# A two-layer hybrid trunk: calmer splitting ahead and top-k, a warmer start, and two embedding blocks moved between the last output products

## The chip, the cores and the metric

The kernel runs on one core of one Trainium2 chip. The metric is the device time of one launch in microseconds (us), from the chip's own timing. The kernel before takes 2018.87 us (median of 3 runs, 2017.33 to 2019.59). A core has a matrix engine (TensorE, PE in the profile), a vector engine (VectorE, DVE), an activation engine (ScalarE, ACT), GpSimd (POOL) and SyncE (SP), which here issues nearly all transfers (DMAs). Each engine runs its instructions in the order in which the program lists them.

## What is computed

Two decoder layers on a sequence of 1024 tokens of width 1024, all in float32. In outline:

```
for i in 0, 1:
    y = gla_mixer(x) if i == 0 else dsa_mixer(x)
    x = layer_norm(ALPHA * x + y) * ln_g[i] + ln_b[i]
    x = x + (p[i] @ ple_w[i]) * sigmoid(x @ ple_gate_w[i])

gla_mixer:  q, k, v, z, a = split(x @ w_in)          # 4 heads, chunks of 64 tokens
            g = log_sigmoid(a @ w_a2 + b_a) / 16;  G = cumsum(g) inside a chunk
            A = tril((q exp(G)) @ (k exp(-G)).T);  o = A @ v + (q exp(G)) @ S   # S: running state
            y = (rms_norm(o) * gn_g * silu(z)) @ w_out
dsa_mixer:  q, k, v, z, qi, ki, wi = split(x @ w_in)   # 16 heads, one k and v for all
            score = sum over 8 index heads of relu(qi @ ki.T) * wi, causal
            keep the top min(256, L/4) keys of each query;  attention on them
            y = (o * silu(z)) @ w_out
```

The term `p[i] @ ple_w[i]` is the per-layer embedding (`ple`): 256 by 1024 weights, done in eight blocks of 128 output columns.

## The kernel before

**Matmuls in three passes.** To keep float32 accuracy, every operand is split into a high part (rounded to the matrix engine's `fp32r`) and a low part (the rest): ACT makes the high part by a copy, DVE the low part by a subtraction (`split`, L395 and L403; for weights `Weights.step`, L180 and L182). A product is then three matmuls, high x high, low x high and high x low. A matmul is 128 by 128 weights against 512 columns.

**Weights.** `Weights` walks one list of keys, `seq`. A key's 128 x 1024 piece is loaded into one of two `wst` buffers (`loads`), split into the tiles `whi` and `wlo` (four buffers each) and handed out by `take`. The weights of layer 1 are used in both halves; `split_ahead` (L203 to L229) splits them once, during layer 0, in pieces of 512 columns: load into `pst` (two buffers), ACT copies to `phi` (L219), SP stores `phi`, DVE subtracts in place (L223), SP stores `pst`. Later the finished parts are simply loaded (`whole`).

**Halves and heads.** The sequence is cut into two halves of 512 tokens. Layer 0 goes through half 0 and half 1, each with four heads (`g_phase` makes the decays from log and exponential functions, `v_phase`, `qk_phase`, the core with its masks `Af`, `Ah`, `Al`, then `out_phase` with its sums in `y`), then the norm (`norm_steps`), the transposes and gate of `tail`. Between the halves stands the small head work of layer 1 for half 0 (`small_head`, `small_kv`, and the index scores with tiles `ix`, `rl`, `sc`). Layer 1 goes through the halves with 16 attention heads; in each head's slot stand projections (`q`, `z`) and output products (`o`) as cover for the softmax and its transposes (`sq`, `PT`, `ph`), whose sums are in the tile `o`. The last output products (`last_outs`, L333) need the last head's result `u`.

**What sets the order.** Nothing here is ordered by hand row by row. `Flow` keeps an estimated clock that is moved on by each matmul. A piece of side work is put in a heap with a due time (`at`, `after`, `chain`), or is fed by a pacer each time its gap has passed: `W.pace` for weights, `bg` for top-k (`topk_steps`) and rope tables, `bg3` for `split_ahead`, `feed_by` for the pieces of x. When the estimated clock passes a due time, the instruction is written into its engine's program at that place. So a different gap, a different `chain` time or a step issued earlier moves instructions against each other on DVE, ACT and SP, and each engine then runs them in that order whether or not the operands are there.

Of the kernel before, what the change touches and what calls it, by code (L numbers as in the profile page):

```python
# [23 lines left out]
HT = 512  # L24
# [113 lines left out]
class Weights:  # L138
# [15 lines left out]
    def step(self):  # L154
# [48 lines left out]
    def split_ahead(self, keys, pool):  # L203
# [11 lines left out]
        for i, (key, c) in enumerate(cuts):  # L215
# [49 lines left out]
def trunk_kernel(ctx, tc, x_tok, x_T, p_T, pos, freq, g_q, g_k, g_v, g_z, g_a, g_a2, g_ba, g_gn, g_o,  # L265
# [28 lines left out]
    def tail_keys(layer):  # L294
        return ([(("p", layer, c), ple_c[layer, c]) for c in range(2)]
                + [(("t", layer, b), gate_c[layer, b]) for b in range(NK)])
# [36 lines left out]
    last_outs = [("o", (6,), 1), ("o", (7,), 0), ("o", (7,), 1)]  # L333

    def unit_keys(u):
        if u[0] == "o":
            return [(("do", j, u[2]), d_o[j // 2, u[2], j % 2]) for j in u[1]]
# [156 lines left out]
    def g_phase(u, A):  # L494
# [16 lines left out]
        def soft(d):  # L511
            def f():
                act.activation(ta[:, d], ta[:, d], AF.Exp, scale=-1.0)
                act.activation(ta[:, d], ta[:, d], AF.Ln, bias=1.0)
            return f
# [29 lines left out]
        chain((0, lambda: None), (0.6, soft(0)), (1.1, soft(1)), (0.3, scan(0)), (1.1, scan(1)),  # L545
              (0.8, middle), (1.9, decays))
# [193 lines left out]
    def accumulate(parts, U, y, ch, rs=None, norm=None, ahead=1):  # L740
# [5 lines left out]
        for t, b in order:  # L746
# [16 lines left out]
            if norm is not None:  # L763
                norm(t)
            yield

    def out_phase(u, y, norm=None):
# [4 lines left out]
        for ch in range(2):  # L772
            parts = [W.take(("o", u["h"], ch, 0)), W.take(("o", u["h"], ch, 1))]
            for i, _ in enumerate(accumulate(parts, U, y, ch, u["rs"], norm if ch else None)):
# [14 lines left out]
    def norm_steps(y, np_, eps):  # L789
# [6 lines left out]
        def norm(t):  # L796
# [14 lines left out]
            chain((0, stats), (2.0, apply))  # L811
        return norm, f_done

    def tail(layer, Pt, y, y_done, final, tp, xps, x_alloc, tmp):

        ple = [tp.tile([128, 4, HT], F32, tag="z", name="ple", bufs=2) for _ in range(2)]
# [13 lines left out]
        for c in range(2):  # L830
            hi, lo = W.take(("p", layer, c))
            for b in range(4):
                ps = pbank()
                n = 0
                for k in range(2):
                    ph, pl = Pt[k]
                    bs = slice(k * 512 + b * 128, k * 512 + b * 128 + 128)
                    for l, r in ((hi, ph), (hi, pl), (lo, ph)):
                        mm(ps, l[:, bs], r, n == 0, n == 5)
                        n += 1  # L840
                    if k == 0:
                        yield
                if c:
                    dve.tensor_copy(ple[c][:, b], ps)
                else:
                    act.activation(ple[c][:, b], ps, AF.Copy)
                yield
                if c == 1:
                    xpose(2 * b)
                    yield  # L850
                    xpose(2 * b + 1)
                    yield
        for b in range(NK):
            def ev(ps, b=b):
                sg = tmp()

                def gated():
                    dve.tensor_mul(sg, sg, ple[b // 4][:, b % 4])
# [270 lines left out]
    def start_half(half):  # L1129
# [9 lines left out]

        def feed():  # L1140
            load(0, 1)
            W.loads(W.ns + 1)
            load(1, 1)
            W.loads(W.ns + 2)
            for k in range(2, NK, 2):
                load(k, 2)
            if half == 0:
                nc.sync.dma_start(ba, g_ba)
# [3 lines left out]
            else:  # L1152
                yield
# [10 lines left out]
        return X, units, feed()  # L1164
# [583 lines left out]
```

## Time and profile before

| | before |
|---|---|
| median of 3 runs | 2018.87 us |
| the profiled execution | 2016.59 us |
| its span, first to last instruction | 2014.8 us |
| mean granted clock of TensorE | 0.993 |
| busy: PE, DVE, ACT, POOL | 97%, 74%, 52%, 3% |

The profiled execution lies 2.3 us below the median and 1.8 us above its span. The granted clock has two levels, 1.2 and 2.4 GHz, written as 0.5 and 1.0 in the records, so that a stretch with a mean of 0.83 has spent a third of its time at the lower one. A row of the timeline gives the start, the busy time of one instruction (or of a run of equal ones), the engine, the line, the operation, the tiles, and in brackets the idle time of the engine before it with what ended it.

### The profile page before, as it was taken

What the parts mean: (1) busy time and instruction counts of PE and PEld (TensorE: products, weight loads), DVE (VectorE), ACT (ScalarE), POOL (GpSimd) and SP (SyncE); (2) the same over time, 40 slices, a digit from 0 to 9 for tenths busy, and PEclk for the clock granted to TensorE, in tenths of its full rate; (3) what the DMA queues carried; (4) which work ended last, traced back from release to release, by engine and by line L of the source; (5) the groups of instructions that cost most, each with busy time, mean ns of one, the idle gap of its engine ahead of it and who ended that gap; (6) DMA issues with size and microseconds to landing.
All of it is one profiled execution on the core that took longest, in us unless ns stands there. A gap on an engine that the chain in (4) does not pass through costs nothing.

```text
span 2014.8 us, 26716 instructions
## 1 busy us (share of the span) xinstructions
PE 1963.4 (97%) x9016; PEld 1616.3 (80%) x9016; DVE 1487.6 (74%) x3037; ACT 1046.5 (52%) x1943; POOL 53.7 (3%) x111
## 2 busy tenths in 40 slices
PE   8999999999999999999999999999899999999999
PEld 6788788877777888888888887888778888888877
DVE  5667666687677797877867986777796887777863
ACT  5664646445465646464555676766442553434432
POOL 0000000010000000000100000000000000000000
PEclk9999999999999999999999999999999999999999
DMA  4557575657856565657667487877766998888864
GB/s 149 174 162 221 171 218 171 222 174 243 283 180 224 161 225 167 225 162 224 196 218 266 157 311 246 303 265 276 271 211 215 352 333 295 291 300 279 295 249 147
DMA packets 173947, 464.96 MB, mean 231 GB/s; under 512 B 20081, under 2 KB 20849, under 8 KB 167665
## 3 DMA queue, kind: packets, MB, share of 16 engines
q1 hardware_dynamic: 173808, 463.25, 68.4%
q8 instruction: 71, 1.16, 0.2%
q14 instruction: 68, 0.55, 0.1%
HBM read 331.18 MB, written 131.99 MB: 230 GB/s over the span
## 4 chain that ended last, share of the span: by engine, by line
PE 81%; DVE 7%; ACT 5%; DMA 4%; issue 2%; SPq 0%; POOL 0%; POOLq 0%; ACTq 0%; DVEq 0%
PE pb L58 59%; PE o L58 8%; PE U L58 6%; PE S L58 5%; DMA xst<-x2s 1%; DMA wls<-pst 1%; DMA pst<-in_d_o 1%; DVE bn L803 1%; PE oT L62 1%; PE tr L58 1%; DVE wlo L182 1%; DVE sc L1018 1%; ACT whi L180 0%; DMA wst<-in_g_v 0%; DMA wlo<-wls 0%
## 5 line engine op out<-in xcount | busy, mean ns | idle before, releaser
L58 PE MATMUL pb<-x,whi 128*128 128x512 f32 x2272 | 709.9, 394 | 3.3 <-ACT whi L180 2.0
L58 PEld LDWEIGHTS pb<-x,whi 128*128 128x128 f32 x2272 | 417.2, 188 | 84.4 <-ACT whi L180 2.8
L58 PE MATMUL pb<-x,wlo 128*128 128x512 f32 x1136 | 444.2, 391 | 0.4 <-DVE wlo L182 0.4
L58 PE MATMUL pb<-whi,u 128*128 128x512 f32 x1024 | 347.2, 399 | 7.6 <-DVE u L395 4.2
L58 PEld LDWEIGHTS pb<-x,wlo 128*128 128x128 f32 x1136 | 213.8, 188 | 48.1 <-DVE wlo L182 2.3
L58 PEld LDWEIGHTS pb<-whi,u 128*128 128x128 f32 x1024 | 194.8, 190 | 49.9 <-DVE u L395 5.0
L58 PE MATMUL pb<-wlo,u 128*128 128x512 f32 x512 | 202.3, 395 | 0.0
L182 DVE TENSOR_TENSOR wlo<-wst,whi 128x512 fp32r<-128x512 f32 x232 | 154.8, 684 | 56.2 <-ACT whi L180 56.0
L180 ACT ACTIVATE whi<-wst 128x512 fp32r<-128x512 f32 x232 | 136.4, 621 | 47.2 <-DMA wst<-in_g_z 13.7
L219 ACT ACTIVATE phi<-pst 128x512 fp32r<-128x512 f32 x130 | 81.4, 626 | 126.2 <-DMA pst<-in_d_z 40.8
L1435 ACT ACTIVATE sq<-P,mx 128x128 f32<-128x128 f32 (+7 forms) x128 | 99.0, 774 | 83.8 <-DVE mx L1428 56.5
L1481 ACT ACTIVATE ph<-PT 128x512 fp32r<-128x512 f32 (+1 forms) x160 | 93.7, 601 | 65.7 <-PE o L58 50.4
L58 PE MATMUL S<-kT,q 128*128 128x512 f32 (+2 forms) x576 | 121.8, 343 | 0.0
L1479 DVE TENSOR_TENSOR PT<-PT,ph 128x512 fp32r<-128x512 f32 (+1 forms) x160 | 101.5, 648 | 20.6 <-ACT ph L1481 20.6
L58 PEld LDWEIGHTS S<-kT,q 128*128 128x128 f32 x576 | 100.6, 188 | 17.8 <-DVE mx L1428 0.7
L58 PEld LDWEIGHTS pb<-wlo,u 128*128 128x128 f32 x512 | 97.6, 191 | 18.8
L223 DVE TENSOR_TENSOR pst<-pst,phi 128x512 fp32r<-128x512 f32 x130 | 89.1, 685 | 29.8 <-ACT phi L219 29.8
L1084 ACT ACTIVATE tk<-sc,tki 128x768 f16<-128x768 f32 (+2 forms) x90 | 92.9, 1032 | 22.0 <-DVE tki L1093 15.9
L58 PE MATMUL o<-ph,vT 128*128 128x512 f32 (+2 forms) x384 | 102.4, 351 | 0.0
L1441 DVE STREAM_TRANSPOSE sq<-sq 128x128 f32<-128x128 f32 (+7 forms) x128 | 97.6, 768 | 3.1 <-ACT sq L1435 3.0
L58 PE MATMUL pb<-whi,x 128*128 128x512 f32 x256 | 89.1, 407 | 10.0 <-ACT whi L180 6.0
L709 ACT ACTIVATE junk<-o 128x512 bf16<-128x512 f32 x32 | 19.1, 597 | 139.8 <-DVE ot L707 135.3
(311 smaller groups left out, 3383.9 us busy)
## 6 DMA issues: line engine op xcount, KB each, us to landing
whi<-whs SPq DMA_DIRECT2D x130, 512.0 KB
wlo<-wls SPq DMA_DIRECT2D x130, 512.0 KB
sqd<-sq SPq DMA_DIRECT2D x192, 256.0 KB
PT<-sqd SPq DMA_DIRECT2D x48, 1024.0 KB
whs<-phi SPq DMA_DIRECT2D x130, 256.0 KB
wls<-pst SPq DMA_DIRECT2D x130, 256.0 KB
wst<-in_g_v SPq DMA_DIRECT2D x32, 512.0 KB
wst<-in_g_z SPq DMA_DIRECT2D x32, 512.0 KB
```

Of the source, the lines that this page charges most:

```text
L58: self.pe.matmul(out, lhsT, rhs, start=start, stop=stop)
L62: self.pe.transpose(out, in_, ident)
L180: self.nc.scalar.activation(hi[:, c], st[:, c], AF.Copy, scale=1.0 if gain is None else gain)
L182: self.nc.vector.tensor_sub(lo[:, c], st[:, c], hi[:, c].bitcast(F32))
L219: self.nc.scalar.activation(hi, st.bitcast(F32), AF.Copy)
L223: self.nc.vector.tensor_sub(st, st.bitcast(F32), hi.bitcast(F32))
L803: dve.bn_stats(st8[:, t, c], y[:, t, c * 512:c * 512 + 512])
L1084: act.activation(junk()[:, :n], scs[j], AF.Sign, bias=cand[:, j:j + 1].bitcast(F32), accum_out=cnt[:, j:j + 1])
L1435: act.activation(to, rows, AF.Exp, scale=-1.0, bias=mx, accum_out=sm[:, t:t + 1])
L1441: dve.transpose(x, x)
L1479: dve.tensor_sub(lo, lo.bitcast(F32), hi.bitcast(F32))
L1481: chain((0, lambda: act.activation(hi, lo.bitcast(F32), AF.Copy)), (0.8, second))
```

## The change

- **Start.** The first piece of x is split first, then the first two weight pieces in full (four steps of `W`, one before), and 22 matmuls of the identity by itself are put on PE ahead of the first real one. The bias tables of DVE come later.
- **`split_ahead`** issues the load of the next piece one step earlier. Its gap is 2.02 instead of 2.1, 2.43 while a core runs and 1.72 while a head's projections run; it stops while the small head work begins.
- **`g_phase`**: both exponentials, then both logarithms, instead of one pair after the other; the scans and decays are due a little later.
- **`norm`** is called for both column halves of `y`: the statistics of the first half are taken as soon as it is complete, not both at the end.
- **The `ple` of layer 1**: blocks 0 and 1 run as a unit of their own between the last two heads' output products; their weights lie in the two `wst` buffers. `tail` then makes six blocks instead of eight and ends with two more bare transposes.
- **Start of half 1**: x is loaded in four transfers of 512 KB spaced by 5 us of the estimated clock instead of five in a row together with two weight pieces, and is split from a later step on, at a gap of 2.2 instead of 1.2.
- **Top-k of half 1's rows**: gap 1.6 becomes 1.5 or 1.75, by the head; a pause is put at the last head. The product `z*inv` is made one group of the attention sum earlier, and the inputs of `ple` are loaded one head earlier.

```diff
             if not whole:
                 self.loads(n + 1)
-            self.parts[n] = tuple(self.pool.tile([128, 1024], F32R, tag=t, name=t, bufs=4) for t in ("whi", "wlo"))
+            tags = (("wst", 2),) * 2 if self.seq[n][0][:3] == ("p", 1, 0) else (("whi", 4), ("wlo", 4))
+            self.parts[n] = tuple(self.pool.tile([128, 1024], F32R, tag=t, name=t, bufs=b) for t, b in tags)
...
             self.nc.scalar.activation(hi, st.bitcast(F32), AF.Copy)
+            nxt = load(*cuts[i + 1]) if i + 1 < len(cuts) else None
             yield
             self.nc.sync.dma_start(there[0][:, c], hi.bitcast(F32))
-            nxt = load(*cuts[i + 1]) if i + 1 < len(cuts) else None
             self.nc.vector.tensor_sub(st, st.bitcast(F32), hi.bitcast(F32))
...
-    last_outs = [("o", (6,), 1), ("o", (7,), 0), ("o", (7,), 1)]
+    last_outs = [("o", (6,), 1), ("p",), ("o", (7,), 0), ("o", (7,), 1)]
...
-        chain((0, lambda: None), (0.6, soft(0)), (1.1, soft(1)), (0.3, scan(0)), (1.1, scan(1)),
-              (0.8, middle), (1.9, decays))
+        chain((0, lambda: None), (0.6, exps), (1.2, logs), (2.2, scan(0)), (0.7, scan(1)),
+              (1.0, middle), (1.9, decays))
...
+            dve.bn_stats(st8[:, t, ch], y[:, t, ch * 512:ch * 512 + 512])
+
             def stats():
-                for c in range(2):
-                    dve.bn_stats(st8[:, t, c], y[:, t, c * 512:c * 512 + 512])
                 dve.bn_aggr(mv[:, t], st8[:, t])
...
+        def fetch():
+            for k in range(0, NK, 2):
+                load(k, 2)
+                yield
...
             next(feeder)
-            W.step()
+            fl.need(lambda: X.t[0] is not None)
+            for _ in range(4):
+                W.step()
             next(feeder)
             feed_by(feeder, 0.0, 0.0)
+            idle = pp.tile([128, 512], F32, tag="o", name="o")
+            for _ in range(22):
+                nc.tensor.matmul(idle[:, 0:128], ident, ident, start=True, stop=True)
...
-                    bg3.set(W.split_ahead(later, lp), 2.1)
+                    bg3.set(W.split_ahead(later, lp), 2.02)
...
+            bg3.gap = 2.43
             steps = core_steps(u)
...
+            bg3.gap = 2.02 if h == GH - 1 else 1.72
...
+            nxt = start_half(1)
+            feed_by(nxt[3], fl.now + 2.0, 5.0)
+            bg3.due = max(bg3.due, fl.now + 7 * B)
...
-                    if i == 8:
-                        feed_by(nxt[2], fl.now + 0.7, 1.2)
+                    if i == 12:
+                        feed_by(nxt[2], fl.now + 0.7, 2.2)
...
-        bg.set(topk_steps([4, 5, 6, 7], scs, l1, tk, tk, on_act=(1, 2, 3)), 1.6)
+        bg.set(topk_steps([4, 5, 6, 7], scs, l1, tk, tk, on_act=(1, 2, 3)), 1.52)
...
+    def ple_block(parts, b, Pt, out, engine):
+
+        hi, lo = parts
+        ps = pbank()
+        n = 0
+        for k in range(2):
+            ph, pl = Pt[k]
+            bs = slice(k * 512 + b * 128, k * 512 + b * 128 + 128)
+            for l, r in ((hi, ph), (hi, pl), (lo, ph)):
+                mm(ps, l[:, bs], r, n == 0, n == 5)
+                n += 1
+            if k == 0:
+                yield
+        if engine is dve:
+            dve.tensor_copy(out, ps)
+        else:
+            act.activation(out, ps, AF.Copy)
+        yield
...
+        turns = iter(range(NK))
+        for b in range(done, 8):
+            if b % 4 == 0 or b == done:
+                parts = first if b < 4 and first else W.take(("p", layer, b // 4))
+            yield from ple_block(parts, b % 4, Pt, ple[b], dve if b >= 4 else act)
+            if b >= 4 + done // 2:
+                for _ in range(2):
+                    xpose(next(turns))
                     yield
...
+    def ple_unit(st):
+
+        st["pw"] = W.take(("p", 1, 0))
+        st["ple"] = [small_tile("qf") for _ in range(2)]
+        for b in range(2):
+            yield from ple_block(st["pw"], b, Pt, st["ple"][b], act)
...
+                if g == len(groups) - 2:
+                    z, inv = get(("z", h), ("inv", h))
+                    dve.tensor_mul(z, z, inv)
+                    st["zs", h] = z
...
+            bg.gap = 1.75 if h > 3 and h % 4 < 2 else 1.5
...
-            if h == 15:
-                Pt = load_p(1, half, lambda: small_tile("q", F32R, 4), 14.0)
+            if h == 14:
+                Pt = load_p(1, half, lambda: small_tile("q", F32R, 4), dur + 2.5)
```

How the rows move is shown at three places. The first is DVE at the start of half 1, in the first head's `k` projection (`m` is k times its decay, which the transposes `tr` on PE read; `pst` is the subtraction of `split_ahead`; `tkj` and `tki` belong to top-k). Before:

```order
L182 TENSOR_TENSOR wlo<-wst,whi 128x512
L1040 TENSOR_SCALAR tkj,tkf<-sc_103,tki 128x384
L223 TENSOR_TENSOR pst<-pst,phi 128x512
L589 TENSOR_TENSOR m<-pb,m 128x512
L658 COPY_PREDICATED Af_91<-cmask,tr 128x128
L631 SCALAR_TENSOR_TENSOR S<-R_97,mid,S 128x512
```

And now:

```order
L594 TENSOR_TENSOR m<-pb,m 128x512
L224 TENSOR_TENSOR pst<-pst,phi 128x512
L183 TENSOR_TENSOR wlo<-wst,whi 128x512
L1109 TENSOR_TENSOR tki<-tkf 128x2
L1110 SCALAR_TENSOR_TENSOR tki<-tki 128x2
L1112 TENSOR_SCALAR tki<-tki 128x2
L183 TENSOR_TENSOR wlo<-wst,whi 128x512
L1059 TENSOR_SCALAR tkj,tkf<-sc_103,tki 128x384
L594 TENSOR_TENSOR m<-pb,m 128x512
```

The subtraction stood directly ahead of the second `m`; now it stands directly behind the first, seven rows earlier.

The second is SP at the end of the small head work (`y` is the buffer that x is loaded into, `in_x_T` the input, `wst<-in_g_v` the first weights of half 1). Before:

```order
L1138 DMA y<-in_x_T 128x512
L199 DMA wst<-in_g_v 128x1024
L1138 DMA y<-in_x_T 128x512
L199 DMA wst<-in_g_v 128x1024
L1138 DMA y<-in_x_T 128x2x512 x3
L963 DMA v<-rope_s 32x512
L964 DMA v<-rope_s 32x512
```

And now:

```order
L1157 DMA y<-in_x_T 128x2x512
L168 DMA whi<-whs 128x1024
L168 DMA wlo<-wls 128x1024
L1157 DMA y<-in_x_T 128x2x512
L982 DMA v<-rope_s 32x512
L983 DMA v<-rope_s 32x512
L200 DMA wst<-in_g_v 128x1024 x3
```

The loads of x have moved up between the weights of the small head (two of the four stand in these rows), and the weights of half 1 come behind the rope tables instead of in the middle of the loads of x.

The third is the last head of layer 1's first half. On PE, the end of the attention sum (`o`) and the first output products that read that head's `u`. Before:

```order
L58 MATMUL o<-ph,vT_9801 128x4x64
L58 MATMUL o<-ph,vT_9802 128x4x64
L58 MATMUL o<-PT,vT_9801 128x4x64
L58 MATMUL pb<-whi,u 128x512
L58 MATMUL pb<-wlo,u 128x512
L58 MATMUL pb<-whi,u 128x512 x2
L58 MATMUL pb<-wlo,u 128x512
```

And now:

```order
L58 MATMUL o<-ph,vT_9823 128x4x64
L58 MATMUL o<-ph,vT_9824 128x4x64
L58 MATMUL o<-PT,vT_9823 128x4x64
L58 MATMUL pb<-q,wst 128x512 x6
L58 MATMUL pb<-whi,u 128x512
L58 MATMUL pb<-wlo,u 128x512
```

Six of the embedding's twelve matmuls stand between the sum and the products; the other six stand among the sum's groups. On DVE at the same place, before:

```order
L1040 TENSOR_SCALAR tk,tkf<-sc_9809,tki 128x768
L1524 TENSOR_TENSOR z<-z,inv 128x512
L1533 TENSOR_TENSOR uf<-o,z 128x4x4x32
L1040 TENSOR_SCALAR tk,tkf<-sc_9810,tki 128x896
L395 TENSOR_TENSOR q<-xst,q 128x512 x2
L395 TENSOR_TENSOR u<-uf,u 128x512
```

And now:

```order
L1059 TENSOR_SCALAR tk,tkf<-sc_9831,tki 128x768
L1554 TENSOR_TENSOR z<-z,inv 128x512
L1508 TENSOR_TENSOR PT<-PT,ph 128x2x4x64
L1059 TENSOR_SCALAR tk,tkf<-sc_9832,tki 128x896
L1567 TENSOR_TENSOR uf<-o,z 128x4x4x32
L398 TENSOR_TENSOR u<-uf,u 128x512
```

The count over 896 columns has passed ahead of `uf`, the unsplit result of the head, and the two splits of the embedding's input no longer stand between `uf` and the low part of `u`.

## Rows read from the trace of the kernel before

**Rows 1.** The page's first part: busy time, share, instructions.

```profile
span 2014.8 us, 26716 instructions
...
PE 1963.4 (97%) x9016; PEld 1616.3 (80%) x9016; DVE 1487.6 (74%) x3037; ACT 1046.5 (52%) x1943; POOL 53.7 (3%) x111
```

**Rows 2.** Windows: stretch and length, busy of PE, PEld, DVE, ACT, POOL; PEclk, DMA.

```profile
5.98:12.70 6.72, 5.74 (x13) 3.90 (x14) 5.23 (x9) 5.41 (x10) 0.00 (x0) 1.00 0.85 300
150.00:200.00 50.00, 50.00 (x233) 41.69 (x232) 36.65 (x62) 22.48 (x44) 1.48 (x4) 1.00 0.72 222
58.00:68.00 10.00, 8.03 (x32) 5.37 (x31) 3.95 (x7) 9.65 (x15) 0.00 (x0) 1.00 0.17 45
406.00:416.00 10.00, 7.95 (x34) 6.25 (x33) 7.68 (x13) 3.62 (x8) 0.15 (x1) 0.83 0.40 131
452.00:464.00 12.00, 10.28 (x60) 7.97 (x59) 10.97 (x18) 10.45 (x17) 1.94 (x3) 1.00 0.67 197
540.00:570.00 30.00, 23.77 (x89) 17.76 (x88) 26.09 (x48) 20.21 (x40) 0.00 (x0) 0.89 0.64 218
636.00:646.00 10.00, 6.91 (x25) 5.63 (x26) 6.75 (x13) 3.58 (x7) 0.00 (x0) 0.83 0.92 328
1226.00:1236.00 10.00, 7.84 (x28) 6.07 (x27) 7.83 (x18) 4.39 (x9) 0.00 (x0) 0.83 0.73 251
1398.00:1408.00 10.00, 8.27 (x44) 6.88 (x43) 6.59 (x18) 6.90 (x18) 0.00 (x0) 1.00 0.67 241
1444.00:1464.00 20.00, 13.87 (x55) 10.84 (x54) 14.38 (x28) 1.81 (x4) 0.00 (x0) 0.83 0.82 297
1934.00:1946.00 12.00, 9.94 (x38) 7.63 (x37) 7.89 (x13) 2.69 (x5) 0.00 (x0) 0.86 0.52 213
```

**Rows 3.** Timeline (start, us, engine, line, operation, tiles [idle before]): the start.

```profile
1.09 0.23 DVE L356 TENSOR_SCALAR ident<-negs 128x128 f32<-128x128 int32 x1 [1.09 <-POOL negs L354]
...
7.74 1.29 DVE L395 TENSOR_TENSOR x<-y,x 128x512 fp32r<-128x512 f32 x2
```

**Rows 4.** Timeline: four short transposes on PE.

```profile
406.36 0.60 PE L62 MATMUL oT<-ident,ot 128*128 128x128 f32 x4
```

**Rows 5.** Timeline: the first head's decays on ACT.

```profile
59.98 1.28 ACT L539 ACT_TABLE_LOAD   x1
```

**Rows 6.** Timeline: a late subtraction on DVE in the third core.

```profile
407.81 0.69 DVE L223 TENSOR_TENSOR pst<-pst,phi 128x512 fp32r<-128x512 f32 x1 [1.84 <-ACT phi L219]
```

**Rows 7.** Timeline: the first weights of half 1 on ACT.

```profile
542.08 1.15 ACT L180 ACTIVATE whi<-wst 128x512 fp32r<-128x512 f32 x2 [4.27 <-DMA wst<-in_g_v]
```

**Rows 8.** Timeline: first head of half 1.

```profile
637.08 0.63 ACT L219 ACTIVATE phi<-pst 128x512 fp32r<-128x512 f32 x1 [3.29 <-DMA pst<-in_d_o]
...
638.35 0.68 DVE L589 TENSOR_TENSOR m<-pb,m 128x512 f32<-128x512 f32 x1
```

**Rows 9.** Timeline: top-k in a slot of layer 1.

```profile
1228.79 0.94 ACT L1084 ACTIVATE tk<-sc,tki 128x768 f16<-128x768 f32 x1 [2.11 <-DVE tki L1093]
```

**Rows 10.** Timeline: the last head of layer 1's first half, DVE.

```profile
1448.36 0.69 DVE L1524 TENSOR_TENSOR z<-z,inv 128x512 f32<-128x512 f32 x1
...
1452.43 1.15 DVE L1040 TENSOR_SCALAR_CACHE_REDUCE tk<-sc,tki 128x896 f16<-128x896 f32 x1 [2.58 <-DMA sc<-sc_s]
...
1454.71 0.68 DVE L395 TENSOR_TENSOR u<-uf,u 128x512 fp32r<-128x512 f32 x1
```

**Rows 11.** Waits of PE: line, releaser: us in total, times, longest.

```profile
PE pb L58 <- DVE u L395: 4.2, 1, 4.2
...
PE U L62 <- ACT zz L984: 2.8, 1, 2.8
...
PE U L62 <- ACT x L826: 1.4, 5, 0.7
```

**Rows 12.** Waits of SP's queue, in the same columns.

```profile
SPq L210 <- DMA wls<-pst: 37.6, 30, 4.9
```

**Rows 13.** Lines of ACT: busy, mean ns of one.

```profile
L514 ACT ACT_TABLE_LOAD x16 | 20.5, 1283 | 0.3
```

More of the change, by code (lines that the diff above doesn't have):

```diff
@@ L294, in tail_keys @@
     def tail_keys(layer):
-        return ([(("p", layer, c), ple_c[layer, c]) for c in range(2)]
+        return ([(("p", layer, c), ple_c[layer, c]) for c in range(layer, 2)]
                 + [(("t", layer, b), gate_c[layer, b]) for b in range(NK)])
@@ L509, in g_phase, with exps, logs @@
             dve.tensor_scalar(m[:, d], ps, bb, 0.0, op0=OP.add, op1=OP.min)
-        def soft(d):
-            def f():
+        def exps():
+            for d in range(2):
                 act.activation(ta[:, d], ta[:, d], AF.Exp, scale=-1.0)
+        def logs():
+            for d in range(2):
                 act.activation(ta[:, d], ta[:, d], AF.Ln, bias=1.0)
-            return f
         def scan(d):
@@ L763, in accumulate @@
             if norm is not None:
-                norm(t)
+                norm(t, ch)
             yield
@@ L773, in out_phase @@
             parts = [W.take(("o", u["h"], ch, 0)), W.take(("o", u["h"], ch, 1))]
-            for i, _ in enumerate(accumulate(parts, U, y, ch, u["rs"], norm if ch else None)):
+            for i, _ in enumerate(accumulate(parts, U, y, ch, u["rs"], norm)):
                 if ch:
@@ L794, in norm_steps, with norm @@
         f_done = [False] * 4
-        def norm(t):
+        def norm(t, ch):
             def power():
@@ L810, in apply, with tail @@
                 f_done[t] = True
-            chain((0, stats), (2.0, apply))
+            if ch:
+                chain((0, stats), (1.8, apply))
         return norm, f_done
-    def tail(layer, Pt, y, y_done, final, tp, xps, x_alloc, tmp):
-        ple = [tp.tile([128, 4, HT], F32, tag="z", name="ple", bufs=2) for _ in range(2)]
+    def ple_block(parts, b, Pt, out, engine):
[15 more added lines that the diff above has]
+        yield
+    def tail(layer, Pt, y, y_done, final, tp, xps, x_alloc, tmp, ple=(), first=None):
+        ple = list(ple)
+        done = len(ple)
+        for c in range(2):
+            t = tp.tile([128, 4, HT], F32, tag="z", name="ple", bufs=2)
+            ple += [t[:, i] for i in range(4)]
         X1 = [None] * NK
@@ L828, in xpose @@
             X.put(k, X1[k], x_alloc)
[L830 to L849, printed above, removed]
+        turns = iter(range(NK))
[6 more added lines that the diff above has]
+                    xpose(next(turns))
                     yield
-                    xpose(2 * b + 1)
-                    yield
+        for k in turns:
+            xpose(k)
+            yield
         for b in range(NK):
@@ L1138, in load @@
             nc.sync.dma_start(raw[:, k:k + n], x_T[k:k + n, :, hs].rearrange("k p t -> p k t"))
+        def fetch():
+            for k in range(0, NK, 2):
+                load(k, 2)
+                yield
         def feed():
[L1141 to L1146, printed above, removed]
-            if half == 0:
+            if half == 0:
+                load(0, 1)
+                W.loads(W.ns + 1)
+                load(1, 1)
+                W.loads(W.ns + 2)
+                for k in range(2, NK, 2):
+                    load(k, 2)
                 nc.sync.dma_start(ba, g_ba)
@@ L1281, in trunk_kernel @@
             spread(steps, fl.now + 1.5, 2 * B + 4.5)
-            bg3.due = max(bg3.due, fl.now + 14.0)
-            nxt = start_half(1)
-            next(nxt[2])
             def kv():
                 for i, _ in enumerate(small_kv(0, X, f32t, alloc, tmp, ups, kh, kl, vh, vl, res)):
-                    if i == 8:
-                        feed_by(nxt[2], fl.now + 0.7, 1.2)
+                    if i == 12:
+                        feed_by(nxt[2], fl.now + 0.7, 2.2)
                     yield
@@ L1512, in f @@
             def f():
-                (ph, pl), *z = get(("parts", h, g), *([("z", h), ("inv", h)] if last else []))
+                (ph, pl), = get(("parts", h, g))
                 fl.req(not first or st.get("done", -1) == h - 1, not last or h < 5 or st["out"] >= h - 4)
@@ L1557, in gate_tiles @@
     def gate_tiles(tp):
-        for tag, bufs in (("z", 3), ("qf", 2), ("rt", 2)):
+        for tag, bufs in (("z", 3), ("rt", 2)):
             for _ in range(bufs):
@@ L1670, in trunk_kernel @@
                 bg.due = max(bg.due, fl.now + 11.0)
-            fl.run(unit(u, norm if u == last_outs[-1] else None))
+            fl.run(unit(u, norm if u[1:2] == ((7,),) else None))
         fl.drain()
+        first = st["ple"], st["pw"]
         st.clear()
@@ L1678, in trunk_kernel @@
         tail_gen = tail(1, Pt, y, y_done, lambda b, t, hs=hs: nc.sync.dma_start(out[b * 128:(b + 1) * 128, hs], t),
-                        tp, spsum, lambda k: (next(gx), next(gx)), tmp1)
+                        tp, spsum, lambda k: (next(gx), next(gx)), tmp1, *first)
         fl.run(tail_gen)
```

25 lines of the change are left out of this document (14 added, 11 removed).

## The prediction

> **What bounds the kernel.** I read the busy shares first, then windows over each place where the matrix engine loses time, then the timeline there, and last the waits. The matrix engine is busy for 1963.4 of 2014.8 us, 97% [rows 1]: it is the bound, and no matmul of the reference is taken away here. So nothing can be won but its idle time, 51.4 us, and what it loses at the lower clock. The mean granted clock of 0.993 gives that second loss as 0.007 x 2014.8, about 14 us. Together some 65 us are there to be had.
>
> The windows [rows 2] show where much of it lies. A matmul of 512 columns at full rate takes 50.00 / 233 = 0.215 us. In each window I take the length less PE's busy time, and add the length times one less the clock. 58 to 68: 2.0. 406 to 416: 2.05 + 1.7 = 3.8. 452 to 464: 1.7. 540 to 570: 6.2 + 3.3 = 9.5. 636 to 646: 3.1 + 1.7 = 4.8. 1226 to 1236: 2.2 + 1.7 = 3.9. 1398 to 1408: 1.7. 1444 to 1464: 6.1 + 3.4 = 9.5. 1934 to 1946: 2.1 + 1.7 = 3.7. The first matmuls, 13 of them in 6.72 us, would take 2.8 at full rate: 3.9 lost (the clock column shows 1.00 there, but 0.44 us of busy time a matmul, 5.74 / 13, is twice the full-rate step, so I read it as the lower level). These ten places hold 44.5 us. The reader is to see that a pause of about 2 us costs nearly twice its length: wherever the idle time passed 2 us, except at 58, 452 and 1398 where it was 2.0 and less, the mean clock fell too.
>
> **The change part by part.** Each term is what I take out of its place, with its ends.
>
> *Start*: 2.5 (1.0 to 3.2). In the run before, the third matmul waits for the low part of x, whose subtraction starts only at 7.74 [rows 3], behind two weight splits and bias tables; it now starts as soon as x has come. That alone is about 1.0. The upper end adds the lower clock of the next ten, 10 x 0.215 = 2.2, if the 22 short matmuls raise it in time. Their own price: four short transposes took 0.60 [rows 4], 0.15 each, so 3.3 us at full rate and 6.6 at half; they begin once the identity stands, at 1.09 + 0.23 [rows 3], and end between 4.6 and 7.9, while the first real matmul began at 5.98. They are hidden or up to 1.9 late, and the low value of the term covers that. I take a value near the upper end, because the weights' low parts are early too.
>
> *Decays of the first head*: 1.6 (0.5 to 2.0). ACT loads its table at 59.98 and runs five exponentials [rows 5], with the next weight copy behind them, and PE waits. In the new order of ACT that copy stands ahead of the decays. The regrouped exponentials and logarithms save table loads: L514 has 16 of 1283 ns [rows 13], one ahead of each logarithm (four heads, two halves, two parts each), and half of these and of the exponentials' go, about 20 us of ACT. ACT is half idle, so I book nothing for them beyond this place. The Trainium skill ("ScalarE: Activation LUTs", section on table sets) says that one set holds both the exponential and the logarithm, by which the old order would have needed no load between them and the regrouping would save nothing. The rows disagree: there is a load for each logarithm.
>
> *Splitting ahead against the cores*: at 411, 3.7 (1.8 to 3.8), at 639, 4.3 (1.7 to 4.8). At 407.81 DVE had stood idle for 1.84 waiting for `phi` in order to subtract [rows 6], with three other instructions and then `Al` behind it, which PE needs. At 637.08 ACT got its piece from DMA after 3.29 us of waiting; the second `m` of the first head came behind the subtraction, at 638.35 [rows 8], and PE waited for it. In the new order of DVE the subtraction stands ahead of the place at 411 by several rows, and at 639 seven rows earlier. The low ends are those in which DVE is still late by about 1 us and the clock falls less. The calmer gap during the cores takes further subtractions out of them; I count nothing for that.
>
> *Start of half 1*: 7.5 (4.0 to 9.5). ACT waited 4.27 us for the first weights of half 1, until 542.08 [rows 7], because they went out inside a burst of five transfers of x. Behind that copy stood `rl`, for which PE waited, and 20 us later, with DVE busy for 26.1 of 30 us [rows 2], PE waited 2.8 for `zz` [rows 11]. Now the loads of x are spread over the small head's time, the weights go out into a freer queue, and five splits of x and several pieces of splitting ahead leave this stretch. I keep 2 us for what is still waited for.
>
> *Norm*: 0.8 (0 to 1.7) at 452. Taking half the statistics earlier shortens the end of the chain on DVE by four of eight statistics; PE waits there for the normalized `y`.
>
> *Top-k*: at 1230, 3.2 (0 to 3.9), at 1402, 0.8 (-1.0 to 1.7). ACT waited 2.11 us for the candidate and then ran a count [rows 9] ahead of the exponential work, and the next subtraction of `PT` was 2.2 us too late for PE. In the new order the counts stand behind that work at this place. The gaps shift every other count as well.
>
> *Embedding between the last products*: at 1444 to 1464, 7.5 (4.5 to 9.0), at 1934 to 1946, 3.2 (2.0 to 3.7). Here PE waited for the last head's `u`: after `z*inv` at 1448.36 came `uf`, and its low part only at 1454.71, since a count had to wait until 1452.43 for its reloaded scores [rows 10]; the wait for that low part alone is 4.2 [rows 11]. Now 6 of the 12 embedding matmuls, 1.3 us, stand behind the sum, `z*inv` is done a group earlier and the other 6 matmuls fill the gaps of the sum. Against it: the waiting count over 896 columns has moved ahead of `uf`. Its reload is issued three rows earlier, ahead of 1 MB of weights, so I expect it in time; a rival below takes the other view. In the second half no top-k runs, and the term there hangs on nothing but the cover.
>
> *New costs*: the two tails lose 2.7 us of cover each by the moved blocks, and end with transposes for which ACT must split; such waits were 0.7 at the longest [rows 11], so 2 x 0.65 = 1.3 (0 to 2.8). And one new pause of the size of that at 1230, 3.9 (0 to 7.8), because moving the pace of a background stream puts its instructions ahead of others somewhere else; the other slots of layer 1 have the same structure and no rule keeps them clear.
>
> Sum: 2.5 + 1.6 + 3.7 + 4.3 + 7.5 + 0.8 + 3.2 + 0.8 + 7.5 + 3.2 = 35.1, less 5.2, is 29.9. The profiled execution took 2016.59, so 1986.7; it lies 2.3 below the median of the runs, and on that median the prediction is 2018.9 - 29.9 = 1989.0.
>
> **Rivals.** *The stalls only move.* Every term goes to its low end (14.5 in all) and the new costs stay at 5.2: 9.3 gained, 2009.6. For it speaks that the order is written from an estimated clock, so a subtraction taken out of one place falls in another; against it that the five largest places have causes which the new order removes outright (a burst of transfers, a count ahead of `u`).
>
> *The count holds the last head.* If the reload lands at 1452.43 as before, the count ends at 1453.6, and `u` comes at about 1455; PE would reach it near 1451, wait 4 us and lose 1.7 at the lower clock. The gain there is 3.8 instead of 7.5: 1992.7.
>
> *Slower: SP's queue stands still.* The load of the next piece is now issued one step, about 2 us, earlier, and it may go out only when the store of the piece two back has landed. SP already waited 30 times, 37.6 us in all, for that store [rows 12]. If it waits at each of the 130 loads, the weight transfers behind it are late. A late weight costs PE some 2 us and 1.7 at the lower clock. From (35.1 - 1.3 + 4) / 3.7, ten such places, the kernel is slower by more than 0.2%; with twelve it takes 2018.9 - 33.8 + 44.4 = 2029.5. For it speaks the longest of these waits, 4.9; against it that weights are loaded two pieces ahead, and that 37.6 us of such waits now leave no pause of PE outside the ten places that is near 2 us. The Trainium skill ("DMA: Bandwidth & Descriptors", anatomy of one DMA) says that transfer engines wait for no semaphore, the issuing sequencer does, so that one load held back holds everything behind it on SP. The waits on SP's rows agree with that, and by it alone the rival would hold; the rows don't show a weight made late by it.
>
> **How the numbers follow.** Chances: the forecast 0.62, the stalls move 0.14, the count holds 0.14, SP's queue 0.10. About 0.2%, 4 us, is what a measurement of this kernel can tell from no change. Faster holds the forecast, the count and most of the first rival (0.10): 0.86. The same holds the rest of that (0.04) and 0.02 of the last: 0.06. Slower is 0.08. All terms at their high ends, 43.3, with no new costs and a few us of the smaller waits elsewhere would give 1972; low ends with two new pauses, 14.5 - 1.3 - 7.8 = 5.4, give 2013.5. The range is 1972 to 2012.
>
> **What would show it.** Right: PE's busy time the same within a few us and the span shorter by 30; the windows at the same places at 0.95 or more of busy time and a clock of 1.00; the first 13 matmuls done by 10.5; ACT's wait for the first weights of half 1 gone; 16 table loads fewer on ACT; the last head's `u` waited for less than 2 us. Wrong: new pauses of 2 us and more that end with a subtraction of `pst`, with a count or with a weight split, SP's waits for the store well over 37.6 us, or the count over 896 columns waiting past 1450 of the old time.

## The result and the profile after

The changed kernel takes 2045.4 us (median of 4 runs, 2041.2 to 2048.4) against 2018.1 for the kernel before (median of 4): a ratio of 1.0136, 95% interval 1.0114 to 1.0158. It is slower by 1.4%, where 1.5% faster was forecast. One run of the kernel before (3274 us) and one of the last kernel below (3270 us) had a granted clock of 0.56 and are left out throughout.

The page's first lines of the kernel after, to be read beside [rows 1]: the span has grown by 29.2 us, PE's busy time by 14.0 (the short matmuls, and others at the lower clock), and its idle time from 51.4 to 66.6.

```profile
span 2044.0 us, 26810 instructions
...
PE 1977.4 (97%) x9060; PEld 1624.4 (79%) x9060; DVE 1491.4 (73%) x3037; ACT 1022.1 (50%) x1927; POOL 52.7 (3%) x111
```

To see where, I took the start of the same matmul in both traces at nine places and subtracted (negative is earlier than before). This is my own table; each figure is a difference of two starts in a timeline.

| place (start before, us) | after | load put back | load back, gap 2.1 | best |
|---|---|---|---|---|
| 13th real matmul (12.69) | -1.3 | -0.8 | -2.2 | -2.6 |
| first `tr`, half 0, head 0 (86.20) | -5.4 | -5.0 | -6.1 | -6.1 |
| head 3 (383.39) | +5.0 | -5.4 | -8.1 | -7.9 |
| transposes of `y`, tail of half 0 (453.27) | +5.6 | -8.3 | -5.7 | -7.5 |
| first `tr`, half 1, head 0 (635.49) | +10.7 | -8.7 | -10.4 | -12.1 |
| head 3 (935.43) | +26.2 | -4.1 | -11.5 | -14.2 |
| first `sm` of layer 1 (1131.93) | +38.7 | +0.9 | -8.8 | -11.4 |
| transposes of `y`, layer 1, half 0 (1472.74) | +29.9 | -7.8 | -17.7 | -20.0 |
| end of the span (2014.81) | +29.2 | -8.4 | -17.4 | -21.0 |

In the row on layer 1, half 0, the changed kernels have done six matmuls more at that place, because the transposes come later in their order; they are some 1.4 us further ahead there than the row says. The first column has the whole story: 5.4 won by 86 us, 44 lost between there and the end of layer 0, 9.5 won back in layer 1. Layer 0 is where `split_ahead` runs.

Next the windows of the kernel after, in the columns of [rows 2]: two of the places where I had counted a gain (58 and 1256), and between them three where before there was nothing to lose.

```profile
58.00:68.00 10.00, 10.00 (x46) 8.29 (x45) 5.73 (x9) 6.79 (x11) 0.00 (x0) 1.00 0.58 201
270.00:290.00 20.00, 11.20 (x38) 8.53 (x37) 8.93 (x16) 6.52 (x12) 0.00 (x0) 0.74 0.61 193
...
520.00:530.00 10.00, 6.04 (x19) 4.50 (x20) 4.88 (x9) 2.46 (x5) 0.00 (x0) 0.66 0.72 257
...
842.00:862.00 20.00, 12.94 (x45) 9.94 (x45) 12.95 (x29) 7.16 (x13) 0.00 (x0) 0.74 0.61 199
...
1256.00:1266.00 10.00, 10.00 (x47) 8.31 (x46) 9.90 (x28) 8.16 (x19) 0.00 (x0) 1.00 0.96 304
```

The decays (58 to 68) and the top-k place (now 1256 to 1266) are filled completely. But 270 to 290 lost 8.8 idle and 20 x 0.26 = 5.2 by the lower clock, and the other two are like it. Before, the same work ran without a gap:

```profile
260.00:290.00 30.00, 30.00 (x137) 24.94 (x136) 20.11 (x34) 12.95 (x24) 0.74 (x2) 1.00 0.75 231
```

The waits say what stands there. SP's wait of the load for the store of two pieces back, in the columns of [rows 12], is ten times what it was:

```profile
SPq L211 <- DMA wls<-pst: 389.9, 121, 6.7
```

This alone says little about time lost. Before, SP stood 249.8 us (95 times) for ACT's copy of `phi`; in the kernel after that wait is 47.0 us (28 times). With its waits for the splits of weights, SP stood some 650 us at these rows before and 720 after: it stands elsewhere rather than longer, and what matters is what stands behind it there. ACT's largest wait, which before did not exist in this form:

```profile
ACT phi L220 <- DMA whs<-phi: 165.3, 64, 8.0
```

And PE's largest waits after, to be read beside [rows 11]:

```profile
PE tr L58 <- DVE m L594: 15.1, 5, 4.2
PE pb L58 <- ACT whi L181: 6.5, 2, 3.9
PE U L58 <- ACT kh L665: 6.4, 3, 2.9
PE pb L58 <- ACT x L406: 6.1, 1, 6.1
```

The timeline shows how one leads to the other. SP's queue before:

```profile
272.03 0.43 SPq L225 DMA_DIRECT2D wls<-pst  x1
272.55 0.38 SPq L221 DMA_DIRECT2D whs<-phi  x1
276.76 0.33 SPq L210 DMA_DIRECT2D pst<-in_d_q  x1
```

And after:

```profile
266.95 0.33 SPq L211 DMA_DIRECT2D pst<-in_d_q  x1
267.39 0.37 SPq L200 DMA_DIRECT2D wst<-in_g_o  x1
267.82 0.42 SPq L223 DMA_DIRECT2D whs<-phi  x1
268.29 0.42 SPq L226 DMA_DIRECT2D wls<-pst  x1
273.64 0.33 SPq L211 DMA_DIRECT2D pst<-in_d_q  x1
...
274.75 0.42 SPq L223 DMA_DIRECT2D whs<-phi  x1
275.23 0.42 SPq L226 DMA_DIRECT2D wls<-pst  x1
280.01 0.33 SPq L211 DMA_DIRECT2D pst<-in_d_q  x1
280.44 0.38 SPq L200 DMA_DIRECT2D wst<-in_g_o  x1
280.91 0.38 SPq L223 DMA_DIRECT2D whs<-phi  x1
```

In both the load waits for the store `wls` to land: 4.7 us before (272.03 to 276.76), 5.4 and 4.8 us after (268.29 to 273.64, 275.23 to 280.01). In the first the store of `phi` has gone out ahead of the waiting load; in the second it stands behind it. There is one `phi` tile, so the next copy waits for that store. The other engines of the kernel after at that moment:

```profile
263.98 0.63 ACT L220 ACTIVATE phi<-pst 128x512 fp32r<-128x512 f32 x1 [3.05 <-DMA whs<-phi]
...
273.11 0.63 ACT L220 ACTIVATE phi<-pst 128x512 fp32r<-128x512 f32 x1 [4.88 <-DMA whs<-phi]
...
279.42 0.63 ACT L220 ACTIVATE phi<-pst 128x512 fp32r<-128x512 f32 x1 [4.46 <-DMA whs<-phi]
279.96 1.32 ACT L181 ACTIVATE whi<-wst,gn 128x512 fp32r<-128x512 f32 x2
...
280.08 0.69 DVE L224 TENSOR_TENSOR pst<-pst,phi 128x512 fp32r<-128x512 f32 x1 [3.70 <-ACT phi L220]
...
280.69 0.68 DVE L594 TENSOR_TENSOR m<-pb,m 128x512 f32<-128x512 f32 x1
...
281.43 0.80 PE L58 MATMUL tr<-ta,m 128*128 128x128 f32 x2 [4.07 <-DVE m L594]
```

The copy of 263.98 was done at 264.61, but its store went out only at 267.82, behind the load that had waited until 266.95; so the next copy waited 4.88 us and ran at 273.11. The turn after it is the same, with less delay in the queue and a wait of 4.46: the weight copies stand behind that copy, DVE waits 3.70 for `phi`, `m` stands behind that, and PE loses 4.07.

### The profile page after: what moved, and what is told of

Its sections match the earlier page's. It is cut to its first block, busy times and chain, and to the rows that moved or that the text cites. A ratio compares the mean times of both kernels' runs of the same rounds, so it can differ in the third digit from the quotient of the medians.

```text
span 2044.0 us, 26810 instructions
## 1 busy us (share of the span) xinstructions
PE 1977.4 (97%) x9060; PEld 1624.4 (79%) x9060; DVE 1491.4 (73%) x3037; ACT 1022.1 (50%) x1927; POOL 52.7 (3%) x111
## 4 chain that ended last, share of the span: by engine, by line
PE 60%; DMA 9%; DVE 9%; ACT 6%; issue 3%; SPq 1%; POOL 0%; ACTq 0%; DVEq 0%; POOLq 0%
PE pb L58 44%; PE o L58 7%; PE S L58 5%; DMA whs<-phi 5%; PE U L58 2%; ACT whi L181 1%; DVE bn L806 1%; DMA wst<-in_g_o 1%; DMA wst<-in_g_k 1%; ACT phi L220 1%; DVE m L526 1%; DVE wlo L183 1%; DVE sc L1037 1%; DVE pst L224 1%; DMA wst<-in_g_q 1%
```

## Experiments

Theory A is what these rows suggest: the one moved line, the load ahead of the store of `phi`, costs layer 0 all it lost. The rivals: B, the new gaps of `split_ahead` crowd its instructions onto the wrong places; C, another part of layer 0.

**The load put back, all else as changed.**

```diff
-            nxt = load(*cuts[i + 1]) if i + 1 < len(cuts) else None
             yield
             self.nc.sync.dma_start(there[0][:, c], hi.bitcast(F32))
+            nxt = load(*cuts[i + 1]) if i + 1 < len(cuts) else None
```

> The changed kernel with one line put back: the load of the next piece of split_ahead is issued behind the store of phi again, as in the kernel before; all other parts of the change stay. Theory A (SP stands still: the load, ahead of that store in SP's program, waits for the landing of the store of two pieces back, and holds the store of phi and the weights behind it): SP's waits of the load for the store fall from 389.9 us to about 40, ACT's phi no longer waits for the store of phi (165.3 now), the pauses of PE in layer 0 go, and the time is 1985 to 2000, so faster than before by 1 to 1.6%. Rival B (the new gaps of 1.72 and 2.43 crowd the subtractions onto the wrong places): the place of the load matters little, 2035 to 2045. Rival C (something else of layer 0, the regrouped decays or the start of half 1): also 2035 to 2045.

Measured: 2006.9 (2006.5 to 2008.2), ratio to before 0.9945 (0.9930 to 0.9959). SP's wait:

```profile
SPq L211 <- DMA wls<-pst: 23.4, 27, 2.3
```

The waits of `phi` for its store are gone. One line is worth 38.5 us. The direction is as theory A had it, and B and C fall as causes of the loss; the size is not, 7 us above its range. The kernel without the fault wins only 11 of the 30 us.

**That one line alone in the kernel before.** The edit is the reverse of the one above, on the old kernel.

> The kernel before with that one line alone: the load of the next piece one step earlier, gap 2.1 as before. Theory A: layer 0 loses what the changed kernel lost there and more, since nothing else is won: 2045 to 2080, SP's waits of the load 300 us and more. Rivals B and C: 2013 to 2025, no change.

Measured: 2042.1 (2040.5 to 2042.9), ratio 1.0118 (1.0100 to 1.0135), 3 us under the range. SP's wait there:

```profile
SPq L210 <- DMA wls<-pst: 401.4, 118, 8.8
```

ACT's `phi` waits for its store here too, 160.3 us in 55 times. The line costs 24 us by itself, and 38.5 in the changed kernel; whether the new gaps make that difference was not tried.

**The early load on GpSimd's queue.**

```diff
-            self.nc.sync.dma_start(st.bitcast(F32), w[key][:, c])
+            self.nc.gpsimd.dma_start(st.bitcast(F32), w[key][:, c])
```

> The changed kernel with the loads of split_ahead issued by GpSimd instead of SP, at the same early place of the program. Theory A: the load waits for the same store, but on GpSimd's queue, where little stands behind it; SP is free, 1985 to 2005, and phi waits at most for its piece. If it is the early load itself (its transfer among others), not SP's standing still: 2030 to 2045.

Measured: 2016.9, one run; neither range. 28 us come back, 10 do not. The wait went to GpSimd, which stood for 355.3 us:

```profile
POOL pst L211 <- DMA wls<-pst: 355.3, 63, 13.6
```

ACT's `phi` still waited for its store 20 times, 37.8 us, which the expectation had ruled out. GpSimd also computes the scale factors of the norms, and those stand behind its waits now. Which of the two makes the 10 us was not tried.

**The store of `phi` on ACT, the load early on SP.**

```diff
-            self.nc.sync.dma_start(there[0][:, c], hi.bitcast(F32))
+            self.nc.scalar.dma_start(there[0][:, c], hi.bitcast(F32))
```

> The changed kernel with the store of phi issued by ACT behind its copy instead of SP; the load stays early on SP. It tells apart the two ways in which SP's standing still can hurt. If by the late store of phi (the one phi tile comes free late, ACT and then DVE's subtraction come late, and what stands behind them): the waits of phi go and the time is 1990 to 2010. If by the weights queued behind the load on SP: phi's waits go, the time stays at 2025 to 2045, with PE waiting for weight splits.

Measured: 2005.9, one run. The two waits:

```profile
SPq L211 <- DMA wls<-pst: 350.7, 119, 6.9
```

```profile
ACT phi L220 <- DMA whs<-phi: 42.4, 24, 3.6
```

This is the experiment that tells most. SP stands still nearly as long as in the changed kernel, with all the weights queued behind the load, and the time is that of the kernel with the load put back. So it is not, in the main, the weights behind the waiting load that cost; it is the store of `phi`, by the single `phi` tile, ACT's order and DVE's. But the store on ACT is worth something by itself (below: 2007.8 to 2002.1 with the load put back), and against that kernel of 2002.1 the early load still costs some 4 us by this one run (the two differ in the short matmuls too, which by themselves are worth nothing: 2006.9 and 2007.8). Two `phi` tiles, which would test the same link directly, were not tried.

**Why only 11 of 30.** With the load put back I varied the rest. First the gaps, 2.1 throughout:

```diff
-                    bg3.set(W.split_ahead(later, lp), 2.02)
+                    bg3.set(W.split_ahead(later, lp), 2.1)
...
-            bg3.gap = 2.43
...
-            bg3.gap = 2.02 if h == GH - 1 else 1.72
```

> The changed kernel with the load put back and the gap of split_ahead at 2.1 throughout, as before (no 2.43 in the cores, no 1.72 in the projections). The kernel with only the load put back takes 2006.9 and gained 11 of the 30 us forecast. Theory A2 (the new gaps put subtractions ahead of other places: the new pauses at 824, 273 and 631 of that kernel are theirs): these pauses go, others come back at the old places 411 and 639, 2000 to 2010. Rival (the gaps are worth their terms, 8 us forecast at 411 and 639): 2010 to 2016.

Measured: 1999.5 (1997.6 to 2006.1), ratio 0.9916 (0.9895 to 0.9936), a little better than the range. The two intervals overlap by a little (0.9930 to 0.9936), and one of the four runs, 2006.1, is close to the kernel with the new gaps. The same pair with 12 short matmuls, below, is clear: 1999.8 against 2007.8, intervals 0.9886 to 0.9919 and 0.9936 to 0.9965. So rival B was right about something, though not about the loss: the new gaps cost some 7 us. With them PE had paused here, behind a subtraction of `split_ahead` and a top-k count (timeline of the kernel with only the load put back):

```profile
821.44 0.63 ACT L220 ACTIVATE phi<-pst 128x512 fp32r<-128x512 f32 x1 [3.32 <-DMA pst<-in_d_z]
...
824.12 0.79 PE L58 MATMUL tr<-ta,m 128*128 128x128 f32 x2 [3.54 <-DVE m L594]
```

That is the fault of 639 before [rows 8] at another head. In the kernel with the gap of 2.1 it is gone, and the pause of 411 is back instead:

```profile
403.24 0.54 PE L58 MATMUL o<-v,Al 128*128 128x512 f32 x1 [2.05 <-DVE Al L398]
```

Then the two gaps apart. Only the calmer cores (the line with 1.72 becomes a plain 2.02):

> The changed kernel with the load put back, gaps of 2.02 and, in the cores, 2.43; the 1.72 of the projections left out. It tells which of the two new gaps costs the 7.4 us between 2006.9 and 1999.5. If the crowding in the projections (1.72) does it: 1998 to 2002. If the calmer cores do: 2005 to 2008.

Measured: 2018.0, one run, outside both. It doesn't tell the two gaps apart, for a reason I had not thought of. Up to the tail of half 1 this kernel is 11.3 us ahead of the one before; then PE stands still once:

```profile
1069.31 1.12 PE L62 MATMUL S<-ident,z 128*128 128x128 f32 x4 [15.37 <-ACT z L951]
```

ACT, ahead of that, in the same kernel:

```profile
1054.66 0.63 ACT L220 ACTIVATE phi<-pst 128x512 fp32r<-128x512 f32 x1 [4.58 <-DMA pst<-in_gate_c]
1059.21 0.63 ACT L220 ACTIVATE phi<-pst 128x512 fp32r<-128x512 f32 x1 [3.92 <-DMA pst<-in_gate_c]
1063.64 0.63 ACT L220 ACTIVATE phi<-pst 128x512 fp32r<-128x512 f32 x1 [3.80 <-DMA pst<-in_gate_c]
1068.14 0.63 ACT L220 ACTIVATE phi<-pst 128x512 fp32r<-128x512 f32 x1 [3.87 <-DMA pst<-in_gate_c]
```

The stream was so slow that its last pieces were left over at the end of layer 0, where `bg3.finish()` writes the rest in one go, ahead of ACT's other work. Each piece then takes a whole turn of load, copy and issue of the store, some 4.5 us. So the 1.72 has a use: it makes up for the 2.43.

Only the quicker projections (no 2.43; 2.02 in the cores, 1.72 in the projections):

> The same with 1.72 in the projections and no 2.43 in the cores (2.02 there). If 1.72 does it: 2005 to 2010. If the 2.43 does: 1998 to 2002.

Measured: 2000.6, one run. By the expectation the calmer cores cost, not the quicker projections, but the traces don't bear that out. At the first `tr` of layer 0's last head (935.43 in the table) the kernel with the 2.43 alone stands at -12.9 and that with the 1.72 alone at -14.8, against -11.5 with 2.1 throughout and -4.1 with both. Neither gap alone makes the pause at 824; the two together put that piece there.

**The start.** Undone altogether (one step of the weights ahead, no short matmuls):

> The changed kernel with the load put back and the start as before (one step of the weights ahead, no short matmuls). In the trace of the kernel with only the load put back, the thirteenth real matmul starts 0.8 us earlier than in the kernel before. If the start is worth what I forecast (2.5): 2009 to 2010, with the thirteenth matmul at 12.7. If the short matmuls give back what they win: 2006 to 2008.

Measured: 2008.0, one run, within 0.1% of 2006.9. And with 12 short matmuls instead of 22:

```diff
-            for _ in range(22):
+            for _ in range(12):
```

> The changed kernel with the load put back and 12 short matmuls at the start instead of 22. If the 22 hold PE until 9.07 while the first weights stand split at 6.1: the first real matmul comes at about 6, the thirteenth 1.5 to 2.5 us earlier than with 22, 2004.5 to 2005.5. If the lower clock then lasts over the first real matmuls: no change, 2006 to 2008.

Measured: 2007.8 (2005.5 to 2009.3), ratio 0.9950 (0.9936 to 0.9965), the same as with 22. The 22 do hold PE: in the kernel with the load put back

```profile
1.38 7.94 PE L1212 MATMUL o<-ident 128*128 128x128 f32 x44 [1.38 <-DVE ident L359]
9.07 0.48 PE L58 MATMUL pb<-whi,x 128*128 128x512 f32 x1
```

they run as 44 instructions of 0.18 us, and the first real matmul starts at 9.07 instead of 5.98. With 12 it starts at 6.51, and the thirteenth at 10.12 instead of 11.90 (13.67 with the start undone). Yet the ends agree: the 1.8 to 3.6 us won at the start are not there at the end. They go at single pauses further on. The kernel with the start undone is 4.0 behind the one with 22 by 280 us; it wins back 1.9 near 633 and 3.8 at the pause of 824, where PE waits 2.42 instead of 3.54 and the clock doesn't fall. The kernel with 12 gives back 2.3 at 275 and 2.5 at 1927, where PE waits 2.20 for a weight from DMA. Why a start moves pauses so far behind it is not shown.

**Towards a better kernel.** The load put back, 12 short matmuls and the store of `phi` on ACT:

> As the one before (load put back, 12 short matmuls) with the store of phi issued by ACT. If the late store of phi still costs something behind SP's other work: a gain of 1 to 3 us over that kernel, 2002 to 2005. If ACT's own issue of 130 stores costs what it wins: the same as that kernel.

Measured: 2002.1 (1998.8 to 2004.2), ratio 0.9922 (0.9904 to 0.9940): better than the 2007.8 (2005.5 to 2009.3) of the same kernel with that store on SP. The same two edits with and without the store on ACT, at the gap of 2.1:

> The changed kernel with the load put back, the gap at 2.1 throughout, 12 short matmuls, and the store of phi issued by ACT. With the load put back, the gap alone gave 1999.5 and the other two together 2002.1, against 2006.9. If the three gains are at different places they add to about 1995. If the store on ACT wins only where the short gap crowds phi: 1998 to 2000.

> The same with the store of phi on SP: 1997 to 1999.5 if the shorter start is worth its 1.8 us at the thirteenth matmul to the end; the difference to the one before is what the store on ACT is worth at the gap of 2.1.

Measured: 1995.6 (three runs, 1994.8 to 1996.6), ratio 0.9885 (0.9868 to 0.9901), with the store on ACT; 1999.8 (1997.9 to 2000.4), ratio 0.9902 (0.9886 to 0.9919), with it on SP. No run of the one is as slow as any of the other, though the intervals overlap. The first is the fastest I have, 1.1% faster than before and 2.4% faster than the changed kernel; it stands in the last column of the table. Its page:

```profile
span 1993.9 us, 26658 instructions
...
PE 1959.3 (98%) x9040; PEld 1612.7 (81%) x9040; DVE 1489.9 (75%) x3037; ACT 1022.3 (51%) x1927; POOL 51.6 (3%) x111
```

## Why the prediction was wrong

**The failed step** is the rival of SP's queue, which I gave a chance of 0.10, priced at 2029.5, and did not put into the sum. The mechanism was named there: the earlier load waits for the landing of the store of two pieces back. Two things were missing.

First its size. I had SP's waits as a total, 37.6 us in 30 times [rows 12], and took "one step, about 2 us, earlier" as a mild change. The wait's size could have been read from the trace of before: at 272.03 the store goes out, at 276.76 the load that needs it starts, 4.7 us. The old place gave the store two steps, 4.2 us, and so the load waited in 30 of 130 cases and shortly; one step gives 2 us and must wait nearly always, for some 3. It waited 121 times, 3.2 us each. The old place seems to have been helped by SP's own wait for ACT's copy, ahead of the load: with the load put back, but the store of `phi` and with it that wait moved to ACT (2002.1), the load waited 83 times, 209.7 us.

Second its way. I looked for late weights behind the load on SP, found none in the rows, and held that against the rival. But the next row of `split_ahead` behind the load in SP's new order was the store of `phi`. I did not ask what waits for that store: the single `phi` tile, so ACT's next copy, so DVE's subtraction, so `m`, `kh` and the weight splits, which stand behind these two in their engines' orders. The store moved to ACT shows that this way costs most of the 38 us; some 4 are left for the early load otherwise, by one run.

**The other terms**, read from the kernel with the load put back. I took the starts of its k-th matmul and of the k-th before (both have 9016 beside the short ones), and read how far the difference moves at each place:

- *Start*: 0.8 instead of 2.5. The first 13 real matmuls took 2.8 us (9.07 to 11.90) instead of 6.7, so the lower clock was gone as I had hoped. But the short ones ran as 44 instructions, where I had counted 22, and their end at 9.0 lies past even the 7.9 that I gave as its upper bound.
- *Decays of the first head*: 3.1 at their place, above the 2.0 of their range, and another 3.0 between 69 and 98, for which I had no term.
- *Splitting ahead against the cores*: the pause at 411 went with the new gaps and came back with the old one, so the term was sized right (3.9 for 3.7). At 639 it was 2.2 for 4.3: the new order lost 1.3 and 0.6 at the neighbours of the old pause. But the pace made a new one at 824, 3.5 idle and 14 x 0.24 = 3.4 by the clock, 6.9 together, where I had allowed 3.9 for one:

```profile
820.00:834.00 14.00, 10.46 (x38) 8.41 (x37) 10.08 (x21) 6.15 (x11) 0.00 (x0) 0.76 0.70 232
```

- *Start of half 1*: 3.8 between the first `ix` and the first `tr` of half 1 instead of 7.5. ACT's wait for the first weights is gone, as forecast, but PE's wait for `zz` [rows 11] is there again, and the clock falls behind it, 20 x 0.17 = 3.4:

```profile
540.00:560.00 20.00, 16.84 (x62) 12.43 (x61) 19.31 (x43) 13.41 (x26) 0.00 (x0) 0.83 0.53 183
```

DVE is busy for 19.3 of 20 us there; I had seen that it was, and moved only ACT's part of the stretch.
- *Norm*: 1.5 lost instead of 0.8 won. The wait for the normalized `y` (0.87 before) is gone, but PE waits 0.96 more for ACT's high part of x and 0.36 for `y` ahead of it; the rest of the 1.5 lies in waits shorter than these.
- *Top-k*: 4.0 at 1230 and 1.9 at 1402, 3.2 and 0.8 forecast. No new pause in the other slots (one of 1.0).
- *Embedding, first half*: 7.3 at the pause, 7.5 forecast, of which 2.2 were lost again in the tail behind it. The rival in which the count holds the last head didn't come: the count over 896 columns ran at 1444.58 without a wait, and the low part of `u` was there as PE came.

```profile
1444.58 1.14 DVE L1059 TENSOR_SCALAR_CACHE_REDUCE tk<-sc,tki 128x896 f16<-128x896 f32 x1
...
1445.29 1.56 PE L58 MATMUL pb<-q,wst 128*128 128x512 f32 x6
...
1448.03 0.69 DVE L398 TENSOR_TENSOR u<-uf,u 128x512 fp32r<-128x512 f32 x1 [1.70 <-ACT u L406]
```

The pause itself went; what I had mis-sized are the tail's new waits, 0.69 for `ple`, 1.20 for `y` and 1.04 for `gx`, for which I had allowed 0.65.
- *Embedding, second half*: 1.5 instead of 3.2, and 1.9 lost again in the tail, so nothing in the end. Here all twelve matmuls of the embedding had run before the end of the sum, and PE waits 1.44 for `u` as it did before; only the clock no longer falls behind that wait (1.00 over 1926 to 1938, 0.86 at the place before [rows 2]). I had shown the order for the first half and carried it over to the second, where more groups make up the sum:

```profile
1932.14 0.40 PE L58 MATMUL o<-ph,vT 128*128 128x256 f32 x2
...
1934.10 0.51 PE L58 MATMUL pb<-whi,u 128*128 128x512 f32 x1 [1.44 <-ACT u L406]
```

- *Table loads*: 16 fewer, as forecast, 8 each left ahead of the exponentials and the logarithms; PE's gain from them is not to be told from that of the decays.
- *New costs*: some 22 instead of 5.2. Beside the pause at 824 (6.5 by this reading) and the tails of layer 1 (2.2 and 1.9), there are a pause of 1.3 idle at 273 (1.6 lost), one of 2.1 at 506 where the small head begins (2.9), waits at 938 and 965 (1.8), the tail of layer 0's second half (3.2), 1.0 in a slot of layer 1 and 0.5 at 671.

So with the load put back the ten terms give 27.0 of the forecast 35.1, another 3.0 came where no term stood, and the new costs are 21.6 where 5.2 was allowed. The difference is the 8.4 of the table (11 by the medians). This is the second step that failed, the size of *New costs*: the rival in which the stalls only move came near the time, 2009.6 for 2006.9, though the terms did not all go to their low ends as it had them. The pauses at 273, 506 and 824 are not there with the gap of 2.1; what makes the waits in the tails and at 938 stays open.

## What to carry to other kernels

When a transfer is issued earlier, measure how long the thing it waits for takes to land, and compare that with the time that the new place leaves; a count of short waits says only that the old place was just early enough. Then read the next row of that queue and follow it: a store behind a waiting load, from a tile with one buffer, holds the engine that fills the tile and all that stands behind it there. And a background stream's pace is two things, which instructions it meets and whether it is finished in time; a slower pace that leaves a remainder pays for it at once.

## What the hardware showed that I had not expected

A store of 256 KB from SBUF to DRAM took 4.7 to 5.4 us from its issue until the load that waited for it went out (272.03 to 276.76, 275.23 to 280.01, 268.29 to 273.64), in kernels that move 227 to 230 GB/s over the span. The float32 identity matmuls of 128 columns ran as two instructions each, 0.18 us an instruction at the start. Issuing 130 stores from ACT cost nothing that the time shows, and won some 4 us at a gap of 2.1 (1999.8 to 1995.6) and 6 at the new gaps (2007.8 to 2002.1).
